# Banded prompt attention with the two key blocks packed into one, and attention traced beside its own projection

## The chip, the cores and the metric

The kernel runs on one NeuronCore of a Trainium2 chip. Its time is what the device takes for one execution, in microseconds (us). TensorE (PE in the profile; PEld is its weight load), VectorE (DVE), ScalarE (ACT) and GpSimd (POOL) compute; SyncE (SP) issues most of the DMA transfers, in order. The four compute engines each run their instructions in a fixed order and meet through semaphores.

## The reference

One inference step of a hybrid decoder layer over a prompt of 2048 tokens (and 8 single decode tokens beside it), model width 1024, in float32:

- n = RMSNorm(x); one projection u = n @ w_in gives for attention q (8 heads of 64), k and v (2 key-value heads of 64), and for the gated linear attention (GLA) q, k, v, an output gate r (512 wide) and a low-rank decay input (16 wide).
- Attention: q and k are RMS-normed per head. A query at position t sees the keys t-127 to t. In blocks of 128 tokens, query i of a block sees key j of its own block if j <= i, and key j of the block before if j > i. The score is q.k/8 plus a bias by distance (one of 32 buckets, per head); a learned sink per head joins the softmax as one more score without a value.
- GLA: a chunked exact recurrence with a data-dependent decay, then a norm per head and multiplication with silu(r).
- h = x + [attention | GLA] @ w_o, then y = h + (silu(z @ w_gate) * (z @ w_up)) @ w_down with z = RMSNorm(h).

The two conditions j <= i and j > i complement each other: for each pair (i, j) exactly one of the two key blocks counts. So 128 scores per query and head carry everything that 256 masked ones carry (in the first block there is no block before).

## The kernel before

The prompt is 16 blocks of 128 tokens (`NB`, `P`). The kernel has stages: A (projection for attention and r, and attention), B (GLA), the output projection, and the feed-forward part. Only stage A changes. Float32 products are made of three products of a high and a low part (`mm3`, lines 102 to 106, hence PE lines 104 to 106 for all dense products); `split` (lines 91 to 93) makes the parts with an ACT copy (line 92) and a DVE subtraction (line 93).

Stage A has these functions:

- `front(b)` loads a block of x, norms it, transposes it on PE and splits it into `nT`; two `nT` buffers exist. It also stores `nT` to DRAM (`nT_d`) for stage B.
- `project(b)` makes q (512 wide) and k, v and decay input (272 wide) with the weights `WA`: 24 PE products for each. q and k are normed (POOL squares, DVE sums, `rstd_fast`), transposed by PE and split into `qT` and `kT`. `kT` holds 256 keys: the own block in its second half, and the block before, copied there by POOL, in its first.
- `project_r(b)` makes r (512 wide) with the weights `WR`: 24 products, then `gate_r` (ACT copy, POOL, three ACT functions, POOL) and a store to `r_d`.
- `attend(b)`, for each of two groups of four heads: scores of 128 queries against 256 keys, two heads to a PSUM bank (`scp`, one bank); DVE adds the bias, which is minus 1e30 outside the band, and takes the maximum (line 360); ACT exponentiates and sums (line 367); POOL divides (line 372). Then for each of the two key blocks PE transposes the four heads' probabilities into a bank (`ppp`, two banks; line 383), `split` takes them to `pT`, and two products with v accumulate in `po` (lines 387 and 388). The result is stored to `mix_d` (line 391). Score buffers `S` are 128 x 1024, three of them; the weight loads at the start use the same buffers for staging.
- `make_bias` builds the bias for 256 keys from 32 buckets at the start, `decode_a` is a generator that does the decode tokens' attention in pieces between the blocks.

The order of the instructions on each engine isn't the traced order as such: a planner orders them by a simulated timeline (`schedule_with_timeline_sim=True`), in which the traced order is the priority. In the loop over blocks (lines 534 to 554) the traced order is front(b+2), project(b+1), project_r(b+1), attend(b); the r products of the last two blocks stand behind the loop. Stage B's buffers lie over those of stage A and come free one by one (`reuse_waits="tile"`). Stage B begins with its own weight loads (`wrq` line 632, `wrb` line 625), the load of `zT` from `nT_d` (line 671) and the q and k products `ps_qk` (line 685) with their copies to `qTb` and `kTb` (lines 687 and 689); later it loads the r blocks from `r_d` (line 741).

## Time and profile before

| what | value |
|---|---|
| median of 3 runs | 2298.53 us (2294.03 to 2301.5) |
| the profiled execution's own time | 2301.44 us |
| its span | 2299.7 us |
| mean granted TensorE clock | 0.984 |
| DMA moved | 364.35 MB |

The page gives for each engine its busy time and share of the span; PE busy isn't PE at its peak, since matmuls are pipelined. Grouped rows read: line, engine, operation, output <- inputs, shape, count, then busy us and mean ns of one, then the idle time of the engine just before them and what ended it. In timelines a row begins with its start and duration in us.

### The profile page before, as it was taken

How to read it: one execution, taken by the hardware profiler on the slowest of the kernel's cores; microseconds unless marked ns; L12 is line 12 of the kernel's file. 1: busy time of each engine (PE TensorE's matmuls, PEld its weight loads, DVE VectorE, ACT ScalarE, POOL GpSimd, SP SyncE). 2: the span in 40 equal slices, each digit the busy share in tenths (PEclk: the TensorE clock that was granted, in tenths of full speed). 3: DMA queues.
4: the chain of work that ended last, by engine and by line, in shares of the span. 5: the costliest groups of instructions: out<-in, count | busy, mean ns of one | idle time of the engine just before them, and what ended most of it. 6: DMA issues, size and time to landing. Idle time of an engine off the chain costs nothing.

```text
span 2299.7 us, 34866 instructions
## 1 busy us (share of the span) xinstructions
PE 2223.9 (97%) x12649; PEld 1921.5 (84%) x12649; DVE 1597.5 (69%) x3241; ACT 955.6 (42%) x2121; POOL 627.8 (27%) x799
## 2 busy tenths in 40 slices
PE   8999998899998899999999999999999999999997
PEld 6888886788887788688888889999999968787886
DVE  6787887588676466766666767666676675748487
ACT  5666777343443233423333323333333243434342
POOL 2443443455465133311110111111010122222222
PEclk9999998999998999999999999999999999999999
DMA  7323334245424699863333357323232378878777
GB/s 240 122 77 111 94 102 157 92 138 171 143 88 184 237 293 317 303 202 110 92 112 94 103 186 277 98 88 107 87 115 88 106 212 174 218 168 218 166 206 239
DMA packets 211225, 364.35 MB, mean 158 GB/s; under 512 B 15428, under 2 KB 128349, under 8 KB 207965
## 3 DMA queue, kind: packets, MB, share of 16 engines
q1 hardware_dynamic: 173996, 258.65, 34.6%
q0 software_dynamic: 37056, 103.47, 17.7%
q8 instruction: 100, 1.64, 0.3%
q14 instruction: 73, 0.59, 0.1%
HBM read 210.98 MB, written 152.16 MB: 158 GB/s over the span
## 4 chain that ended last, share of the span: by engine, by line
PE 81%; DVE 5%; DMA 5%; issue 4%; POOL 2%; ACT 2%; SPq 0%; POOLq 0%; DVEq 0%; ACTq 0%
PE ps_b L105 7%; PE ps_b L104 7%; PE ps_b L106 7%; PE ps_c L105 5%; PE ps_c L104 5%; PE ps_c L106 5%; PE ps_a L105 5%; PE ps_a L104 5%; PE ps_a L106 5%; PE ps_d L104 3%; PE ps_wo L104 3%; PE ps_d L106 3%; PE ps_d L105 3%; PE ps_wo L106 3%; PE ps_wo L105 3%
## 5 line engine op out<-in xcount | busy, mean ns | idle before, releaser
L104 PE MATMUL ps_b<-z,whl 128*128 128x258 f32 (+1 forms) x792 | 254.0, 321 | 1.2 <-ACT whl L92 1.2
L106 PE MATMUL ps_b<-z,whl 128*128 128x258 f32 (+1 forms) x792 | 253.1, 320 | 1.7 <-DVE whl L93 1.7
L105 PE MATMUL ps_b<-z,whl 128*128 128x258 f32 (+1 forms) x792 | 254.3, 321 | 0.0
L92 ACT CAST dm<-mr 128x384 fp32r<-128x384 f32 (+1 forms) x224 | 108.1, 488 | 187.2 <-PE ps_b L106 99.4
L105 PE MATMUL ps_a<-z,whl 128*128 128x258 f32 (+1 forms) x528 | 169.2, 320 | 0.0
L105 PE MATMUL ps_c<-z,whl 128*128 128x258 f32 (+1 forms) x528 | 169.1, 320 | 0.0
L106 PE MATMUL ps_a<-z,whl 128*128 128x258 f32 (+1 forms) x528 | 168.9, 320 | 0.0
L106 PE MATMUL ps_c<-z,whl 128*128 128x258 f32 (+1 forms) x528 | 168.9, 320 | 0.0
L104 PE MATMUL ps_c<-z,whl 128*128 128x258 f32 (+1 forms) x528 | 168.6, 319 | 0.2 <-DMA z<-zc_d_P 0.2
L104 PE MATMUL ps_a<-z,whl 128*128 128x258 f32 (+1 forms) x528 | 168.8, 320 | 0.0
L106 PEld LDWEIGHTS ps_b<-z,whl 128*128 128x128 f32 x792 | 149.4, 189 | 14.5 <-DVE whl L93 2.4
L104 PEld LDWEIGHTS ps_b<-z,whl 128*128 128x128 f32 x792 | 149.4, 189 | 13.1 <-ACT whl L92 1.3
L105 PEld LDWEIGHTS ps_b<-z,whl 128*128 128x128 f32 x792 | 149.3, 189 | 11.9
L93 DVE TENSOR_TENSOR dm<-mr,dm 128x384 fp32r<-128x384 f32 (+1 forms) x224 | 115.1, 518 | 59.6 <-ACT dm L92 59.6
L92 ACT CAST whl<-wrg 128x512 fp32r<-128x512 f32 x132 | 81.6, 619 | 156.7 <-PE ps_b L106 82.2
L802 POOL TENSOR_TENSOR bd<-E,qTb 64x128 f32<-64x128 f32 x224 | 126.7, 566 | 60.7 <-ACT E L787 47.2
L969 DVE TENSOR_TENSOR gu<-ps_c,gu 128x512 f32<-128x512 f32 (+1 forms) x130 | 78.0, 600 | 57.8 <-PE ps_c L106 57.2
L93 DVE TENSOR_TENSOR whl<-wrg,whl 128x512 fp32r<-128x512 f32 x132 | 90.7, 688 | 36.6 <-ACT whl L92 36.3
L1268 POOL DMA_DIRECT2D md_d<-m x22 | 15.6, 711 | 363.8 <-DVE m L1231 363.8
L92 ACT CAST whl<-sy 128x512 fp32r<-128x512 f32 x88 | 54.6, 620 | 134.7 <-PE ps_b L106 84.7
L104 PE MATMUL ps_wo<-WO,mt 128*128 128x512 f32 x256 | 103.6, 404 | 6.9 <-ACT mt L92 6.9
L104 PEld LDWEIGHTS ps_c<-z,whl 128*128 128x128 f32 x528 | 99.8, 189 | 8.6 <-issue 0.6
(390 smaller groups left out, 6669.1 us busy)
## 6 DMA issues: line engine op xcount, KB each, us to landing
mr<-md_d SPq DMA_DIRECT2D x24, 1344.0 KB
zc_d_P<-zhl POOLq DMA_DIRECT2D x56, 512.0 KB, 6.4
z<-zc_d_P SPq DMA_DIRECT2D x14, 2048.0 KB
wrg<-in_w_gate_dram SPq DMA_DIRECT2D x44, 512.0 KB
wrg<-in_w_up_dram SPq DMA_DIRECT2D x44, 512.0 KB
nT_d<-nT SPq DMA_DIRECT2D x16, 1024.0 KB
zT<-nT_d SPq DMA_DIRECT2D x8, 2048.0 KB
h_d<-gu POOLq DMA_DIRECT2D x48, 256.0 KB, 4.6
```

The source lines that it names most:

```text
L92: nc.scalar.copy(h, src)
L93: (eng or nc.vector).tensor_tensor(l, src, h.bitcast(F32), ALU.subtract)
L104: nc.tensor.matmul(ps, lh, rh, start=start, stop=False, skip_group_check=more)
L105: nc.tensor.matmul(ps, lh, rl, start=False, stop=False, skip_group_check=more)
L106: nc.tensor.matmul(ps, ll, rh, start=False, stop=stop, skip_group_check=more)
L802: nc.gpsimd.tensor_tensor(bv[rows, :, h], eo, qo, ALU.mult)
L969: nc.vector.tensor_tensor(out, a, b, ALU.add)
L1268: nc.gpsimd.dma_start(md_d[sb][g][:, :, q, fp - GROUPS[g][0], :], src.rearrange("p (m t) -> p m t", m=4))
```

## The change

1. Scores are packed. After the score products of a pair of heads (still 256 keys wide), a predicated copy on DVE writes, where j > i (`afterQ`), the score of the earlier block's key over that of the own block's key, within the PSUM bank. In the first block it writes minus 1e30 from the tile `none`. Bias, maximum, exponential and division then go over 128 keys in place of 256, and the bias needs no mask.
2. The products with v change: with p the packed probabilities, v the own and v' the earlier values, the sum is p v + (p where j > i)(v' - v). So p is transposed once per head group and split once; POOL multiplies both parts with the mask `afterK` into `pa`; two products use `vp`, two use `dv`, which `project` makes with a POOL subtraction and a split. There are four products per head group, as before.
3. `S` has six buffers of half the size; the weight loads are staged in pieces of 512 elements where they use them. The score pool has two banks, the transpose pool one.
4. The loop's traced order is front(b+1), project(b), attend(b), project_r(b). The r products of blocks 11 to 15 are traced later: 11 in block 13, 12 and 13 in block 14, 14 and 15 in block 15, each behind attend. They load their `nT` again from `nT_d` (1 MB).

```diff
+LATE = (11, {13: (11,), 14: (12, 13), 15: (14, 15)})
...
-        sp = pool(ph, "a_s", 3)
+        sp = pool(ph, "a_s", 6)
...
-        scp = pool(ph, "a_sc", 1, space=PSUM)
-        ppp = pool(ph, "a_pp", 2, space=PSUM)
+        scp = pool(ph, "a_sc", 2, space=PSUM)
+        ppp = pool(ph, "a_pp", 1, space=PSUM)
...
+        def staged_split(hi, lo, src, width):
+            nk = src.shape[1]
+            staged[0] += 1
+            if staged[0] % 2 == 0 and nk * width > 512:
+                wr = wl.tile([P, D], F32, tag="pT", name="wr", bufs=3).rearrange("p (k n) -> p k n", n=width)
+                nc.sync.dma_start(wr, src)
+                split(hi, lo, wr)
+                return
+            step = min(512 // width, nk)
+            for k in range(0, nk, step):
+                wr = sp.tile([P, 512], F32, tag="S", name="wr")[:, 0:step * width].rearrange("p (k n) -> p k n", n=width)
+                nc.sync.dma_start(wr, src[:, k:k + step])
+                split(hi[:, k:k + step], lo[:, k:k + step], wr)
...
+            vraw[b] = vsrc
+            if b:
+                dv = wk.tile([P, 2, HD], F32, tag="dv", name="dv", bufs=1)
+                nc.gpsimd.tensor_tensor(dv, vraw.pop(b - 1), vsrc, ALU.subtract)
+                d4 = dvs[b % 3].rearrange("p v (a d) -> p (v a) d", d=HD)
+                split(d4[:, 0:4:3], d4[:, 1:3], dv)
...
         def project_r(b):
-            pr = dense(nTs.pop(b), P, WR, 0, 512)
+            if b in nTs:
+                nT = nTs.pop(b)
+            else:
+                nT = nTp.tile([P, 2, KD, P], F32R, tag="nT", name="nTr")
+                nc.sync.dma_start(nT.bitcast(F32), nT_d[b // 2][:, :, :, (b % 2) * P:(b % 2 + 1) * P])
+            pr = dense(nT, P, WR, 0, 512)
...
-                St = sp.tile([P, 4, 256], F32, tag="S", name="S")
+                St = sp.tile([P, 4, P], F32, tag="S", name="S")
...
+                    pv = ps.rearrange("p (c a j) -> p c a j", c=2, a=2)
+                    other = pv[:, :, 0] if b else none.unsqueeze(1).to_broadcast([P, 2, P])
+                    nc.vector.copy_predicated(pv[:, :, 1], afterQ.unsqueeze(1).to_broadcast([P, 2, P]), other)
...
-                        nc.vector.tensor_tensor_reduce(St[:, c, k0:], ps[:, o:o + nk], bias[:, h, k0:], 1.0,
+                        nc.vector.tensor_tensor_reduce(St[:, c], ps[:, o + P:o + 256], bias[:, h], 1.0,
...
-                for kt in kts:
-                    ps = ppp.tile([P, 512], F32, tag="pp", name="ps_p")
-                    for c in range(4):
-                        nc.tensor.transpose(ps[:, c * P:(c + 1) * P], S[v][:, c, kt * P:(kt + 1) * P], ident)
-                    pT = wl.tile([P, 2, 512], F32R, tag="pT", name="pT", bufs=3)
-                    split(pT[:, 0], pT[:, 1], ps)
-                    vv = vps_ if kt == 0 else vp
-                    nc.tensor.matmul(po, vv[:, v], pT[:, 0], start=kt == kts[0], stop=False)
-                    nc.tensor.matmul(po, vv[:, v], pT[:, 1], start=False, stop=kt == 1)
+                ps = ppp.tile([P, 512], F32, tag="pp", name="ps_p")
+                for c in range(4):
+                    nc.tensor.transpose(ps[:, c * P:(c + 1) * P], S[v][:, c], ident)
+                pT = wl.tile([P, 2, 512], F32R, tag="pT", name="pT", bufs=3)
+                split(pT[:, 0], pT[:, 1], ps)
+                if b:
+                    pa = wl.tile([P, 2, 512], F32R, tag="pT", name="pa", bufs=3)
+                    for i in range(2):
+                        nc.gpsimd.tensor_tensor(pa[:, i].rearrange("p (c t) -> p c t", c=4),
+                                                pT[:, i].bitcast(F32).rearrange("p (c t) -> p c t", c=4),
+                                                afterK.unsqueeze(1).to_broadcast([P, 4, P]), ALU.mult)
+                for i in range(2):
+                    nc.tensor.matmul(po, vp[:, v], pT[:, i], start=i == 0, stop=i == 1 and b == 0)
+                if b:
+                    for i in range(2):
+                        nc.tensor.matmul(po, dv[:, v], pa[:, i], start=False, stop=i == 1)
...
-            if b + 2 < NB:
-                front(b + 2)
             if 1 < b + 1 < NB:
-                project(b + 1)
-                if b + 1 < NB - 2:
-                    project_r(b + 1)
+                front(b + 1)
+            if b > 1:
+                project(b)
             attend(b)
+            if b >= LATE[0]:
+                nTs.pop(b)
+            elif b > 1:
+                project_r(b)
+            for late in LATE[1].get(b, ()):
+                project_r(late)
...
-        project_r(NB - 2)
-        project_r(NB - 1)
```

What else moves with it: the bias table has 256 columns in place of 384 and is built by two flips in place of four; the masks are loaded as `c_after` (two of 128 x 128); `ks` has three buffers, since v of the block before is needed; the decode tokens' square goes to a `pT` buffer.

More of the change, by code (lines that the diff above doesn't have):

```diff
@@ L216, in hymba_kernel @@
             vps.append(vp)
+        dvs = [pc.tile([P, 2, P], F32R, name=f"dv{i}") for i in range(3)]
+        vraw = {}
         def dense(nT, n, W, c0, c1):
@@ L366, in attend @@
                     h = 4 * v + c
[L367 removed]
+                    nc.scalar.activation(St[:, c], St[:, c], AF.Exp, bias=nm[:, h:h + 1],
                                          accum_out=den[:, h:h + 1])
@@ L1386, in _onehot @@
 def _onehot():
-    m = np.arange(384)
-    dist = 255 - m
-    n = np.maximum(dist, 0)
+    m = np.arange(256)
+    n = (127 - m) % 128
     nf = np.maximum(n, 1).astype(np.float32)
```

85 lines of the change are left out of this document (40 added, 45 removed).

## The prediction

> **What bounds the kernel now.** I read the page's totals first, then the busy time by stretch, then the PE timeline of the one stretch where PE isn't full, then the grouped instructions for prices. The times are of one profiled execution: 2301.44 us, of which the span is 2299.7.
>
> ```profile
> span 2299.7 us, 34866 instructions
> PE 2223.9 (97%) x12649; PEld 1921.5 (84%) x12649; DVE 1597.5 (69%) x3241; ACT 955.6 (42%) x2121; POOL 627.8 (27%) x799
> ```
>
> PE is the busiest engine, but the share is over all stages; the change lies in stage A (prompt projection and attention) alone. In the view by stretch the columns are stretch, length, then busy us of PE, PEld, DVE, ACT, POOL, the granted TensorE clock, DMA share, GB/s:
>
> ```profile
> 60.00:340.00 280.00, 280.00 (x1680) 243.16 (x1679) 226.27 (x634) 199.94 (x550) 121.83 (x115) 1.00 0.33 101
> ...
> 356.00:372.00 16.00, 9.62 (x43) 6.89 (x42) 12.18 (x41) 11.98 (x34) 4.58 (x3) 0.79 0.22 58
> 372.00:390.00 18.00, 13.11 (x87) 11.98 (x88) 16.11 (x42) 15.02 (x39) 8.43 (x4) 0.90 0.84 276
> 390.00:410.00 20.00, 16.50 (x100) 14.09 (x100) 10.64 (x34) 11.40 (x33) 7.71 (x9) 0.92 0.08 28
> ...
> 500.00:600.00 100.00, 95.82 (x620) 84.04 (x619) 81.49 (x181) 43.80 (x104) 54.97 (x80) 1.00 0.51 161
> ```
>
> From 60 to 340 us PE has no idle time at all and DVE, the next, is at 226.3/280 = 81%. So in this body a PE instruction taken away is time gained, and DVE work only counts once it passes PE's. From 356 to 410 PE idles (54 - 39.2 = 14.8 us) and is granted less clock: 9.62 x 0.21 + 13.11 x 0.10 + 16.50 x 0.08 = 4.6 us more. That tail holds 19.4 us which better order can win. What PE does there (start, duration, then the idle time before it in brackets):
>
> ```profile
> 364.04 0.58 PE L355 MATMUL ps_s<-kT,qT 128*128 128x256 f32 x1 [2.27 <-DVE mx L360]
> ...
> 365.06 0.80 PE L387 MATMUL po<-pT,vp 128*128 128x512 f32 x1
> ...
> 371.87 0.39 PE L104 MATMUL ps_qk<-zT,W 128*128 128x264 f32 x1 [0.29 <-DVE qT L315]
> ...
> 374.77 0.28 PE L106 MATMUL ps_qk<-zT,WQ 128*128 128x264 f32 x1
> ...
> 383.23 0.58 PE L355 MATMUL ps_s<-kT,qT 128*128 128x256 f32 x1 [2.99 <-DVE mx L360]
> ```
>
> It runs score products that wait for VectorE to empty the one score bank, with nothing beside them. Why so many attentions are left there, the SP queue shows (issue of each store and load):
>
> ```profile
> 323.58 0.33 SPq L335 DMA_DIRECT2D r_d<-r  x1
> 325.72 0.32 SPq L391 DMA_DIRECT2D mix_d<-o  x1
> ...
> 347.82 0.33 SPq L391 DMA_DIRECT2D mix_d<-o  x1
> ...
> 365.35 0.32 SPq L335 DMA_DIRECT2D r_d<-r  x1
> ...
> 370.34 0.42 SPq L391 DMA_DIRECT2D mix_d<-o  x1
> ...
> 383.52 0.34 SPq L335 DMA_DIRECT2D r_d<-r  x1
> 387.90 0.80 SPq L673 DMA_DIRECT2D lrTb<-lr_d  x2
> 390.35 0.34 SPq L391 DMA_DIRECT2D mix_d<-o  x1
> ...
> 403.41 6.88 SPq L391 DMA_DIRECT2D mix_d<-o  x2
> ```
>
> Of 16 r products only two stores follow the one at 323.58, so 14 are done; of 16 attentions five stores follow 325.72, so 11 are done. The attentions, each traced behind the next block's projection, trail by three blocks, and the tail is made of them.
>
> **The change, part by part.**
>
> ```profile
> 215.14 0.87 PE ps_p L383 x8
> ...
> 223.10 0.23 PE ps_d L105
> ```
> ```profile
> L383 PE MATMUL ps_p<-ident,S x248: 270/272/421, 60.3 to 405.7; 128*128 128x128 f32 x124
> ```
> ```profile
> L104 PE MATMUL ps_d<-WR,nT 128*128 128x512 f32 x106 | 42.2, 398 | 0.0
> L360 DVE CUSTOM_DVE_ANT_0 S<-ps_s,bias,sinkB 128x256 f32<-128x256 f32 x97 | 43.2, 479 | 11.6 <-PE ps_s L356 11.0
> L93 DVE TENSOR_TENSOR pT<-ps_p,pT 128x512 fp32r<-128x512 f32 x48 | 31.8, 683 | 3.1 <-ACT pT L92 2.7
> L93 DVE TENSOR_TENSOR vp<-ks,vp 128x128 fp32r<-128x128 f32 x12 | 7.0, 587 | 3.8 <-ACT vp L92 3.8
> L372 POOL TENSOR_TENSOR S<-S,den 128x1024 f32<-128x1024 f32 x23 | 43.6, 1895 | 70.7 <-DVE den L371 29.5 <-DVE rf_t L125 10.4 <-DVE rf_t L124 10.3
> L240 POOL TENSOR_SCALAR rt<-r 128x512 f32<-128x512 f32 x12 | 18.0, 1496 | 42.0 <-ACT r L239 42.0
> L251 POOL TENSOR_TENSOR sq<-qs 128x512 f32<-128x512 f32 x14 | 15.0, 1074 | 6.6 <-ACT qs L289 6.6
> L241 ACT ACTIVATE rt<-rt 128x512 f32<-128x512 f32 x12 | 7.6, 633 | 1.2 <-POOL rt L240 1.2
> ```
> ```profile
> L360 DVE CUSTOM_DVE_ANT_0 S<-ps_s,bias,sinkB 128x128 f32<-128x128 f32 x8 | 2.4, 339 | 2.6 <-PE ps_s L356 2.6
> L513 PE MATMUL ps_rev<-rev,flip 128*128 128x512 f32 x8 | 4.2, 612 | 0.2 <-DVE bias L514 0.2
> ```
> ```profile
> L815 DVE COPY_PREDICATED AT<-lmask,ps_l 128x512 f32<-128x512 uint8 x41 | 37.0, 902 | 9.1 <-PE ps_l L807 8.9
> ```
>
> *PE.* The durations overlap in the pipe, so PE is priced by spacing, from the chain: eight transposes take 0.87 us (0.109 each), a 512-wide product 0.23. Transposes of the probabilities fall from 248 to 16 x 8 = 128: 120 x 0.109 = **-13.1 us**, in the full body or in the tail. The score products keep their width; the products with values stay four per head group (two with v, two with the differences dv). Halving the bias drops 4 of 8 flip records: between 0 (VectorE work and weight loads set that early stretch) and 4 x 0.612 = -2.4 us; I take **-1**.
>
> *DVE.* 106/8 = 13.25 r products lie in the stretch of those rows, nearly all of the 280 us: a block is 21.1 us of PE, 226.3/13.25 = 17.1 of DVE. Per block the change takes away 8 x (0.479 - 0.339) = 1.1 and two splits of 0.683, and adds one 128x128 subtraction (0.587) and four predicated copies 2x128 wide from PSUM to PSUM, a form the trace lacks. Bounds: 0.339 (the 128-wide reduction) and 0.902 (the 512-wide predicated copy); I take 0.48, the 256-wide PSUM reduction, since the width is that. DVE: 17.1 - 1.1 - 1.4 + 0.6 + 1.9 = 17.1 us (16.6 to 18.8) against PE's 21.1 - 0.9 = 20.2. Cost: nothing, behind PE.
>
> *ACT* loses two 512-wide casts and half of each exponential per block; it stays below its 200/280. *POOL* loses half of two normalisations (1.9 us), gains four 512-wide mask products (4 x 1.07 = 4.3) and a small subtraction: about 121.8/13.25 = 9.2 to 12 us of 20.2. The two mask products stand between the split and the dv products of a head group, 2.1 us in a row; the first two value products don't wait for them. Cover is other blocks' dense products; without cover it is 2.1 us each.
>
> *Staging, constants, buffers.* Weight bytes are the same in smaller pieces, the rev loads shrink from four to two, two 64 KB masks come in, the decode square moves to another pool: zero, give or take 2 us. A second score bank takes away the waits seen at 364 and 383 us; a single transpose bank is emptied in 0.6 + 0.7 us twice per block, far below 20.
>
> *Order.* An attention now stands before the next projection, so at the last projection about one attention is left and not 4.5. r products 11 to 15 come at blocks 13 to 15. Each is 24 x 0.23 = 5.6 us of PE, with the copy, three activations, two POOL steps and the store as before, and a new 1 MB reload of the normalised block on SP. That is 28 us of PE work, independent of attention, to lie under the last chains: the 19.4 us go. What is late next is the last r product's own tail, because stage B's first copies already waited for it:
>
> ```profile
> 381.25 2.24 POOL L244 TENSOR_TENSOR r<-r,rt 128x512 f32<-128x512 f32 x1
> ```
> ```profile
> 389.30 0.68 ACT L687 ACTIVATE qTb<-ps_qk 128x264 f32<-128x264 f32 x2
> ```
>
> The first q product was complete at 375, its copy ran at 389.3, just after the last r buffer was stored (383.5) and freed (387.9): qTb lies over that memory. Now the chain starts when the last r product ends: copy 0.6, POOL 1.5, three activations 1.9, POOL 1.3 to 2.2, store 4.4 = about 10 us. Two q groups (24 in 371.87 to 374.9, 3 us) cover 6. Left over: 4 us, and a stretch at half clock behind it (365.06: 0.80, where a 512-wide product in the body has 0.40) of about 1.5. Net of the tail: -19.4 + 5.5 = **-13.9**.
>
> *Added cost.* Blocks 11 and 12 have no r product: PE 20.2 - 5.6 = 14.6 against DVE's 17.1, 2.5 us each: 0 to +5, I take **+3**. Reloads: SP issues in order, and each waits for a slot of two; behind it queue attention's stores and stage B's weight and zT loads, for which the q products wait.
>
> ```profile
> nT_d<-nT SPq DMA_DIRECT2D x16, 1024.0 KB
> ```
> ```profile
> 343.08 11.61 DMA wrq<-in_w_in_dram
> ```
>
> At 276 GB/s a megabyte takes 3.8 us, less than an r product: 0. At the 11.6 us which the piece in the chain took it is 6 us too long, four times: +24. I take **+2**, since the stretches have DMA room (0.22 to 0.84). Waits in the body from chains placed just in time: 0, as now, to 12 (stage B's 4.2 idle per 100 us, over 280); **+3**.
>
> Sum: -13.1 - 1 - 13.9 + 3 + 2 + 3 = -20. 2301.4 - 20 = 2281.4; the profiled run lies 2.9 above the median 2298.5 of the three shown, so **2278**.
>
> **The rivals.**
>
> *Order as before (0.15).* The instruction order is a planner's, by readiness; tracing attention earlier need not place it earlier. Then the tail stays and 14 us of PE work go: 2284. For it: score products already break into the middle of dense groups. Against: the three blocks of lag match the traced order.
>
> *POOL blocks VectorE (0.13).*
>
> ```profile
> L261 DVE TENSOR_TENSOR qn<-qs,rf_y x16: 674/691/2290, 25.5 to 351.2; 128x512 f32<-128x512 f32 x16
> ```
>
> One form goes from 0.67 to 2.29 us. If each of the four mask products and the subtraction delayed a DVE instruction by its own length (4.8 us a block), DVE were at 21.9 and would pass PE's 20.2: 11 blocks x 1.7 + 2 x 7 = 33 us in place of the 6 for waits and blocks 11 and 12, so -20 + 27 = +7, 2305; half of the 33, more likely, -20 + 10 = -10, 2288. Against: the median is 0.69, so most aren't delayed. The Trainium skill, SBUF — State Buffer, section SBUF: two separate sides, states such a lock: a GpSimd instruction and a VectorE one with two SBUF inputs exclude each other for the whole instruction. The maximum in the row agrees, the median says how seldom it bites.
>
> *Slower: PE waits in each block (0.14).* Attention now stands ahead of the next projection in the order PE must keep. If in each block one product waits on the longer DVE-ACT-POOL chain as at 364.04 (2.27 us, then some 1.7 of half clock), that is 4 us x 14 = 56 in place of my 3: -20 + 53 = +33, 2331. It decides from 23/14 = 1.6 us per block on. For it: two mask products and a predicated copy lie in the chain. Against: PE waits for nothing in 280 us now, with the same engines behind it.
>
> **How the numbers follow.** The forecast has 0.58: with nothing added and no wait for the last r it would be -35 (2264), with waits of 12, blocks of 5 and half the reload bound -2, so its own range is 2264 to 2294. What a measurement can tell from no change is 0.3%, 6.9 us. Faster: 0.50 of the forecast, 0.15 of the first rival, 0.06 of the second: 0.71. Same: 0.07 + 0.06: 0.13. Slower: the third rival's 0.14 and 0.01 of each of the two. The range to 2301 takes in most of the second rival and leaves out the slower one.
>
> **What would show it.** 128 transposes of S; no PE idle in the body, blocks of about 20 us; the r stores 11 to 15 behind the 13th attention's, at most two mix stores after the last projection; a q-copy wait of about 4 us. Wrong would be: PE waits on pa or den in mid-body, a predicated copy near 0.9, PE waiting on the reload, DVE over 90%.

## The result, and the profile after

The changed kernel takes 2318.76 us (median of 4 runs, 2315.1 to 2325.28), the kernel before 2299.04 beside it: a ratio of 1.0082, 95% interval 1.0064 to 1.01. It is slower by 19.7 us, where 20 us less were forecast. The profiled execution took 2315.1 us, the fastest of the four, so the two profiles read here lie 13.7 us apart and not 19.7. Of all runs in this document one, of e16, ran in a slower state of the chip (2438.13 us at a granted clock of 0.842), and e16's numbers leave it out.

The page's totals of the changed kernel:

```profile
span 2313.3 us, 34767 instructions
...
PE 2215.2 (96%) x12525; PEld 1907.2 (82%) x12525; DVE 1605.9 (69%) x3294; ACT 933.0 (40%) x2111; POOL 685.2 (30%) x874
```

PE has less work, as planned: 12525 instructions, 124 fewer, and 8.7 us less busy time. So the loss is in waiting and in the slower clock beside it. Four stretches of stage A in the view by stretch (stretch, length, busy us of PE, PEld, DVE, ACT, POOL, granted clock, DMA share, GB/s), the kernel before first and the changed one behind it:

```profile
40.00:100.00 60.00, 59.53 (x330) 48.07 (x329) 45.29 (x134) 41.68 (x115) 26.01 (x27) 1.00 0.43 130
100.00:250.00 150.00, 150.00 (x903) 130.52 (x902) 118.39 (x333) 103.02 (x281) 65.55 (x63) 1.00 0.30 92
250.00:340.00 90.00, 90.00 (x551) 79.36 (x550) 76.69 (x215) 68.32 (x189) 39.37 (x37) 1.00 0.35 108
340.00:430.00 90.00, 74.81 (x405) 61.63 (x404) 62.71 (x184) 55.60 (x145) 34.43 (x35) 0.91 0.46 147
```
```profile
40.00:100.00 60.00, 50.91 (x240) 37.61 (x240) 37.69 (x111) 35.22 (x95) 25.90 (x28) 0.86 0.34 102
100.00:250.00 150.00, 148.09 (x867) 127.28 (x866) 121.22 (x375) 95.58 (x289) 86.63 (x92) 1.00 0.31 98
250.00:340.00 90.00, 82.31 (x480) 71.08 (x480) 80.78 (x234) 58.50 (x180) 52.21 (x58) 0.96 0.33 104
340.00:430.00 90.00, 72.05 (x385) 60.87 (x385) 59.49 (x162) 49.99 (x136) 47.93 (x45) 0.92 0.58 178
```

I read such a row as *lost time*: length minus PE's busy time, plus busy time times what the clock lacks to 1. For the first row of the changed kernel that is 9.1 + 0.14 x 50.9 = 16.2 us. By stretch:

| stretch | before | after |
|---|---|---|
| 40 to 100 | 0.5 | 16.2 |
| 100 to 250 | 0 | 1.9 |
| 250 to 340 | 0 | 11.0 |
| 340 to 430 | 21.9 | 23.7 |
| sum | 22.4 | 52.8 |

30.4 us more are lost, and 13.1 us of work are gone: 17.3 us net. Where stage A ends shows the same. The groups of the first value product of stage B (the start of the first and the last stand behind the durations), before and after:

```profile
L104 PE MATMUL ps_v<-WV,zT x128: 388/396/795, 410.4 to 715.8; 128*128 128x512 f32 x128
```
```profile
L106 PE MATMUL ps_v<-WV,zT x128: 388/395/629, 428.2 to 729.8; 128*128 128x512 f32 x128
```

It comes 17.8 us later. At the last value product 14.0 us are left (729.8 against 715.8); how stage B wins back the rest wasn't followed. So there are two new holes, one at the start, one from 250 us on, and the old hole at the end of stage A is as large as it was.

*The hole from 250 us on.* PE's longest waits from 250 to 430 us in the changed kernel (who waited for what: sum, times, longest), and two of them in PE's timeline:

```profile
PE ps_d L106 <- DMA nTr<-nT_d: 8.4, 2, 5.0
PE ps_s L380 <- ACT kT L344: 5.3, 3, 3.1
PE ps_k L340 <- DVE kn L283: 3.8, 2, 2.1
PE po L420 <- DVE pT L95: 3.5, 1, 3.5
```
```profile
349.85 0.80 PE L106 MATMUL ps_d<-WR,nTr 128*128 128x512 f32 x1 [5.04 <-DMA nTr<-nT_d]
365.58 0.50 PE L106 MATMUL ps_d<-WR,nTr 128*128 128x512 f32 x1 [3.35 <-DMA nTr<-nT_d]
```

The r products that were to fill the end wait for their own reload, and run slowly behind the wait (0.80 for a product that takes 0.39). SP's queue shows when the reloads (`nTr`) were issued:

```profile
306.71 0.53 SPq L297 DMA_DIRECT2D nT_d<-nT  x1
312.63 0.59 SPq L358 DMA_DIRECT2D nTr<-nT_d  x1
...
343.53 0.59 SPq L358 DMA_DIRECT2D nTr<-nT_d  x1
344.57 1.81 SPq L297 DMA_DIRECT2D nT_d<-nT  x1
346.47 3.89 SPq L361 DMA_DIRECT2D r_d<-r  x1
...
359.26 0.58 SPq L358 DMA_DIRECT2D nTr<-nT_d  x1
```

The first reload goes out at 312.6 and the second at 343.5, 31 us apart. The buffers are the two that the last blocks' norms also use. PE starts its last projection product with block 13 at 312.31 and with block 14 at 343.22, so each of these reloads goes out as a projection lets go of its buffer; the other way round, ACT begins block 15's norm at 332.0, just after PE has read the first reloaded block (331.1). The last projection ends at 383.5, by when three of the five late r stores (346.47, and others at 367.54 and 380.42) have gone, and PE ends the fifth late r product at 396.6, before the last block's first score product at 399.69: these r products ran ahead of the last attention and not beside it.

*The hole at the start.* PE's timeline there, start, duration, then idle time in brackets and what ended it:

```profile
75.14 0.47 PE L420 MATMUL po<-pT,vp 128*128 128x512 f32 x1 [1.47 <-ACT rt L256]
...
79.26 1.22 PE L420 MATMUL po<-pT,vp 128*128 128x512 f32 x2 [1.39 <-DVE o L425]
...
83.63 1.02 PE L141 MATMUL ps_nT<-ident,xtd 8*128 8x8 f32 x8 [1.04 <-DVE xtd L136]
85.77 1.11 PE L141 MATMUL ps_nT<-ident,xt 128*128 128x128 f32 x4 [1.12 <-DVE nTdec L95]
```

No dense product stands between these: PE has run out of normed blocks, because the next block's transposes come behind the decode tokens' (`xtd`). A smaller part of the 16.2 us lies before that: PE waits for the load of the bias to be flipped, which is issued at 42.28 us where the first of these loads went out at 36.06 before. PE's row of that wait in the kernel before, in the changed one and in e17 (below):

```profile
48.94 1.13 PE L513 MATMUL ps_rev<-rev,flip 128*128 128x512 f32 x2 [0.16 <-DVE bias L514]
```
```profile
46.02 1.58 PE L552 MATMUL ps_rev<-rev,flip 128*128 128x512 f32 x2 [2.86 <-DMA rev<-ext_d]
```
```profile
46.82 1.10 PE L557 MATMUL ps_rev<-rev,flip 128*128 128x512 f32 x2 [3.20 <-DMA rev<-ext_d]
```

The prediction had PE waiting on the reload among its signs of being wrong; the hole at the start it hadn't named.

### The profile page after: what moved, and what is told of

The parts are those of the page before. It is cut to its first block, busy times and chain, and to the rows that moved or that the text cites. A ratio compares the mean times of both kernels' runs of the same rounds, so it can differ in the third digit from the quotient of the medians.

```text
span 2313.3 us, 34767 instructions
## 1 busy us (share of the span) xinstructions
PE 2215.2 (96%) x12525; PEld 1907.2 (82%) x12525; DVE 1605.9 (69%) x3294; ACT 933.0 (40%) x2111; POOL 685.2 (30%) x874
## 3 DMA queue, kind: packets, MB, share of 16 engines
q0 software_dynamic: 37056, 103.47, 17.7%
## 4 chain that ended last, share of the span: by engine, by line
PE 62%; issue 16%; DVE 7%; POOL 7%; DMA 5%; ACT 2%; SPq 1%; POOLq 0%; DVEq 0%; ACTq 0%
PE ps_b L107 5%; PE ps_b L106 5%; PE ps_b L108 5%; PE ps_c L107 4%; PE ps_c L106 4%; PE ps_c L108 4%; POOL h_d L1406 4%; PE ps_a L107 3%; PE ps_a L106 3%; PE ps_a L108 3%; PE ps_wo L106 3%; PE ps_wo L108 3%; PE ps_wo L107 3%; PE ps_d L106 2%; PE ps_d L108 2%
```

## The experiments

Times are medians, ratios are against runs of the kernel before beside them, whose medians were 2299.8 to 2301.0.

### Which part costs: e1 to e4

e1: arithmetic, buffers and banks of the changed kernel, the loop's traced order of before.

```diff
-            if 1 < b + 1 < NB:
-                front(b + 1)
-            if b > 1:
-                project(b)
+            if b + 2 < NB:
+                front(b + 2)
+            if 1 < b + 1 < NB:
+                project(b + 1)
+                if b + 1 < NB - 2:
+                    project_r(b + 1)
             attend(b)
...
+        project_r(NB - 2)
+        project_r(NB - 1)
```

> Packed keys, buffers and banks of the changed kernel, but the traced order of the kernel before (next block's projection and r product ahead of each attention, the last two r products behind the loop, nothing reloaded). If the new order is what loses time, PE is busy without a gap again from 60 us to the last projection, the 120 transposes are gone, the tail stays: about 2299 - 13 = 2286. If the packed arithmetic loses it (predicated copies, POOL masks, VectorE and POOL blocking each other), PE waits in the body here too: 2305 to 2320.

Measured: 2294.41 us, ratio 0.9972 (0.9962 to 0.9982). It lies between the two expected times.

e2: the changed kernel, each r product with its own block.

```diff
-LATE = (11, {13: (11,), 14: (12, 13), 15: (14, 15)})
+LATE = (16, {})
```

> The changed kernel with every r product right behind its own attention, none late and none reloaded. If the late r products cost more than they fill (8.4 us of waits for the reload, VectorE-bound blocks 11 and 12, about 11 us of lost PE time from 250 to 340 us), this is 5 to 15 us faster than the changed kernel, 2304 to 2314, and the 16 us lost before 100 us stay. If they do fill the tail, it is slower than the changed kernel by 10 us or more, about 2330.

Measured: 2300.25 us, ratio 1.0 (0.999 to 1.0009). Late r products cost 18.5 us in place of filling the end, more than the 5 to 15 expected.

e3: the changed kernel, in which blocks 0 and 1 are projected in the loop as the others are, so that no two attentions follow each other at the start.

```diff
-        project(0)
-        project(1)
-        project_r(0)
-        project_r(1)
         dec = decode_a()
...
-            if b > 1:
-                project(b)
+            project(b)
```

> The changed kernel, but the first two blocks go through the loop like the others (projection, attention, r product), in place of two projections and two r products ahead of two attentions in a row. If the 16 us of PE time lost from 40 to 100 us come from the two attentions in a row with too little dense work beside them, most of it goes: 2305 to 2310. If they come from the decode piece or from the loads at the start, the time stays at 2319.

Measured: 2322.45 us, ratio 1.0097 (1.0082 to 1.0112). The hole at the start doesn't come from the two attentions in a row.

e4: the arithmetic, buffers and banks of before with the order, the late r products and their reload as in the change.

```diff
+LATE = (11, {13: (11,), 14: (12, 13), 15: (14, 15)})
...
-            if b + 2 < NB:
-                front(b + 2)
             if 1 < b + 1 < NB:
-                project(b + 1)
-                if b + 1 < NB - 2:
-                    project_r(b + 1)
+                front(b + 1)
+            if b > 1:
+                project(b)
             attend(b)
+            if b >= LATE[0]:
+                nTs.pop(b)
+            elif b > 1:
+                project_r(b)
+            for late in LATE[1].get(b, ()):
+                project_r(late)
```

> The kernel before with nothing changed but the traced order: front, projection, attention, r product of the same block, five r products late with a reload; 256 keys, old buffers and banks. If the order is what loses time, the loss of about 33 us shows here without the 13 us that packing saves: 2325 to 2335. If the packed arithmetic is what loses it, the order gains as forecast: 2280 to 2290.

Measured: 2322.92 us, ratio 1.0097 (1.0082 to 1.0112). That is just under the range expected if the order loses the time. The order with its late r products costs some 23 us with either arithmetic. So the loss comes with the order, and the packing as it stands in e1 wins 6.5 us, less than its 14 us of PE work; e9 below shows why.

### The hole at the start: e5, e6, e9, e10, e12

e5 is e1, e6 the changed kernel, with the decode pieces begun one block later.

```diff
-            if b >= 1:
+            if b >= 2:
                 next(dec, None)
```

> The packed arithmetic in the order of before (2294.4 us), with one edit: the decode tokens' pieces begin after block 2 in place of block 1. Nothing is left out. Theory: the loss of about 9 us between 60 and 100 us comes from the first decode piece, whose square now takes a pT buffer, waits there for the packed block's last products, and holds the next block's norm behind it on ScalarE; by then two more blocks are in flight and the wait is covered. Then the loss in that stretch falls from 9.0 to under 3 us and the time to 2286 to 2289. Rival: the packed chain itself is too long for the first blocks, whatever stands beside it; then the loss stays at 7 to 10 us and the time at 2292 to 2296.

> The changed kernel (2318.8 us) with the same edit: the decode pieces begin after block 2. Theory, the decode piece is what starves TensorE at the start: the loss between 40 and 100 us falls from 16 to under 7 us and the time to 2308 to 2311. Rival, the start starves because only one block is normed ahead (front of b+1, not of b+2): the loss stays at 12 to 17 and the time at 2315 to 2320.

Measured: e5 2298.45 (0.9996, 0.9983 to 1.0009), e6 2320.27 (1.0088, 1.0072 to 1.0105). Neither theory: nothing was won, but the hole moved with the piece. In e5 nothing is lost from 60 to 100 us any more and 11.6 us from 100 to 150; in e6 9.7 us are lost from 40 to 100 and 10.8 from 100 to 250, in place of 16.2 and 1.9. So it belongs to the decode piece, wherever that stands.

The next three put its square back where it was, into a score buffer: e9 is e1, e10 the changed kernel and e12 is e2 with this edit.

```diff
-                sqd = wl.tile([P, D], F32, tag="pT", name="sqd", bufs=3)
+                sqd = sp.tile([P, D], BF16, tag="S", name="sqd")
```

> The packed arithmetic in the order of before (2294.4 us), with the decode tokens' square put back among the score buffers S (stored as bfloat16, so that it fits into one; nothing reads it). Nothing is left out. With the decode pieces begun a block later the loss of 9 us at 60 to 100 us moved to 100 to 150 (0.0 and 11.6), so it belongs to the decode piece. Theory A, it is the square's wait for a pT buffer: the loss between 40 and 150 us falls from 12.8 to under 5 us and the time to 2286 to 2290. Theory B, it is VectorE's and ScalarE's full order around the piece, whatever the buffer: the loss stays at 9 to 15 us and the time at 2292 to 2297.

> The changed kernel (2318.8 us) with the decode square back among the score buffers S. Theory A (the square's pT buffer): the loss between 40 and 150 us falls from 18 to under 9 us, the time to 2307 to 2312. Theory B (the order around the piece): 2315 to 2321.

> The changed kernel without late r products (2300.3 us) and with the decode square among the S buffers. Theory A (the square's pT buffer): 2289 to 2293. Theory B: 2297 to 2302. The difference to the old order with the same edit is the price of attention ahead of the next projection: some 6 us if the two effects add.

Measured: e9 2285.21 (0.9935, 0.9918 to 0.9951), e10 2306.82 (1.0029, 1.0019 to 1.004), e12 2292.09 (0.9963, 0.995 to 0.9976). Theory A in all three, in e9 and e10 just below its range: 9.2, 12.0 and 8.2 us won. The square's own group (count, durations, first and last start) in the changed kernel, and then in e10:

```profile
L133 ACT ACTIVATE sqd<-xtd x1: 1051/1051/1051, 78.4 to 78.4; 8x1024 f32<-8x1024 f32 x1
```
```profile
L133 ACT ACTIVATE sqd<-xtd x1: 1052/1052/1052, 63.8 to 63.8; 8x1024 bf16<-8x1024 f32 x1
```

It takes the same 1.05 us and starts 14.6 us earlier. The edit changes the buffer (and the type of an output that nothing reads); so what counts is the ring it is in, here the three `pT` buffers, which the attentions fill with `pT` and `pa` at that time. ACT has no idle time just ahead of the square at 78.4: it stands late in ACT's order. That the planner put it there because a `pT` buffer came free late fits all this, but isn't shown directly. Right behind it on ACT stands the next block's norm (79.44 us, in e10 64.86), and behind that the transposes on PE. e10 loses, by this row, 2.9 us from 40 to 100 in place of 16.2, all of it the wait for the flip's load (the second row is for the late r products below, as is the third):

```profile
40.00:100.00 60.00, 57.13 (x334) 46.90 (x333) 49.23 (x155) 42.12 (x122) 32.22 (x34) 1.00 0.42 130
...
250.00:340.00 90.00, 78.81 (x453) 67.88 (x452) 82.03 (x250) 58.68 (x187) 52.16 (x57) 0.93 0.41 124
340.00:430.00 90.00, 77.44 (x380) 64.76 (x380) 54.57 (x140) 45.49 (x113) 42.28 (x43) 0.88 0.55 172
```

One thing stays open: e4 keeps the square in one of three full-size score buffers and has a hole of 12.8 us from 60 to 100 us too. Its square starts at 72.3 us, earlier than in the kernel before (77.5), which has no hole there; so a late square alone doesn't explain it, and nothing else was tried.

### The late r products: e7, e8, e17

e7 is the changed kernel with only the r products of blocks 14 and 15 late, from normed blocks that stay in SBUF.

```diff
-LATE = (11, {13: (11,), 14: (12, 13), 15: (14, 15)})
+LATE = (14, {})
...
-            if b >= LATE[0]:
-                nTs.pop(b)
-            elif b > 1:
+            if 1 < b < LATE[0]:
                 project_r(b)
...
+        project_r(NB - 2)
+        project_r(NB - 1)
```

> The changed kernel, but r of blocks 11 to 13 stays with its block, and only the r products of blocks 14 and 15 are traced behind the loop, with their normed blocks still in SBUF: no reload, no block without an r product before the 14th. Nothing is left out. Without any late product the time was 2300.3. Theory A, the late products cost through the reload (8 us of waits on it) and the stretches without r: the time is 2293 to 2301, since two r products cover part of the 16 us which TensorE loses at the end. Rival B, any r product behind the last attention delays the memory that the next stage needs: 2305 to 2315.

Measured: 2302.02 us, ratio 1.0009 (0.9999 to 1.0019), the same as without late products (e2). It is just above theory A's range. Two late products without a reload cost next to nothing, and win nothing.

e8 has all five behind the last attention.

```diff
+LATE = (11, {15: (11, 12, 13, 14, 15)})
```

> The changed kernel with all five late r products (11 to 15, reloaded) traced behind the last attention, none between the last projections. Nothing is left out. Theory A, the five cost because blocks 11 to 15 without r products are bound by VectorE and then each waits on a reload that goes through the two buffers one after the other: the time is 2318 to 2332, with the loss between 250 and 390 us larger than in the changed kernel (about 25). Rival B, they cost because they ran ahead of the last projections and so covered nothing: 2300 to 2308.

Measured: 2308.85 us, ratio 1.0037 (1.0026 to 1.0048): 9.9 us under the changed kernel, 8.6 over e2, just past rival B's range. So both theories held half: that three of them ran ahead of the last projections, with their reloads, was some 10 us of the cost, and 8.6 remain when they don't. Its row from 250 to 340 us shows a loss that isn't a wait on the reload, for e8 issues its first reload at 336 us:

```profile
250.00:340.00 90.00, 80.51 (x478) 69.26 (x477) 82.34 (x239) 58.27 (x182) 52.50 (x57) 0.96 0.32 99
```

It loses 12.7 us there, and the changed kernel 11.0. These blocks have no r product beside them. So a reload that comes late costs in two ways: PE waits for it, and more blocks go without an r product.

e17 is e10, in which the reloads of blocks 11, 12 and 14 have a buffer of their own, in the memory that the decode work has left.

```diff
-                nT = nTp.tile([P, 2, KD, P], F32R, tag="nT", name="nTr")
+                if not late_pool:
+                    late_pool.append(pool(ph, "a_nTr", 1))
+                nT = (late_pool[0].tile([P, 2, KD, P], F32R, tag="nTr", name="nTr") if b in (11, 12, 14)
+                      else nTp.tile([P, 2, KD, P], F32R, tag="nT", name="nTr"))
```

> The changed kernel with the decode square among the S buffers (2306.8 us), with an own buffer for the reloaded blocks 11, 12 and 14 (in the memory that the decode tokens' work has left by then), while 13 and 15 reload into the two buffers as before. Nothing is left out. Theory A, TensorE loses 8.8 us of waits on the reload, and some 5 more of clock behind them, because the reload queues for the two buffers which the last norms use: the waits fall under 2 us and the time to 2294 to 2299. Theory B, the late products cost because they run ahead of the last projections and so hold up the last chains, whenever they are loaded: 2303 to 2309.

Measured: 2285.88 us, ratio 0.9942 (0.9926 to 0.9959). 20.9 us under e10, far more than theory A's 8 to 13. PE's longest waits from 250 to 430 us in e17 (the reload is none of them), its first two reloads in SP's queue, and its rows by stretch:

```profile
PE ps_s L385 <- ACT kT L344: 6.8, 3, 4.7
PE ps_v L781 <- ACT v L777: 1.4, 1, 1.4
```
```profile
266.07 0.59 SPq L363 DMA_DIRECT2D nTr<-nT_d  x1
...
308.99 0.59 SPq L363 DMA_DIRECT2D nTr<-nT_d  x1
```
```profile
250.00:340.00 90.00, 85.79 (x510) 74.44 (x509) 80.75 (x256) 58.73 (x191) 55.17 (x60) 1.00 0.48 141
340.00:430.00 90.00, 79.99 (x477) 67.47 (x476) 68.27 (x165) 48.70 (x120) 57.22 (x65) 0.96 0.58 186
```

The first reload goes out at 266 us, an r product is there from 300 us on to stand between the waits, and what is lost falls from 16.7 to 4.2 us (250 to 340) and from 21.9 to 13.2 (340 to 430): 21.2 us, as much as the medians differ (20.9; the two profiles differ by 24.0). Of it 9.5 us are idle time of PE (11.2 + 12.6 in e10, 4.2 + 10.0 here; e10's waits on the reload were 8.8), and 11.6 are clock (0.07 x 78.8 + 0.12 x 77.4 = 14.8 in e10, 0.04 x 80.0 = 3.2 here). So by these rows the slower clock cost rather more than the idle time.

Against e12, which has no late products, e17 wins 6.2 us by the medians; the intervals of the two ratios overlap a little. So much the five late r products are worth when their reload doesn't share the norms' buffers.

### What the packing is worth: e11, e14, e13

e11 is e9 with the banks of before, e14 the kernel before with the banks of the change.

```diff
-        scp = pool(ph, "a_sc", 2, space=PSUM)
-        ppp = pool(ph, "a_pp", 1, space=PSUM)
+        scp = pool(ph, "a_sc", 1, space=PSUM)
+        ppp = pool(ph, "a_pp", 2, space=PSUM)
```

e14's edit is the reverse one.

> As the run of the old order with the square among the S buffers, and with one score bank and two transpose banks, as before the change. Theory, the second score bank wins what TensorE waits for VectorE's score maxima: with one bank the time is 4 to 10 us longer than with two. Rival, the single transpose bank costs as much as the second score bank wins: within 3 us of it.

> The kernel before, with one edit: two score banks and one transpose bank in place of one and two. Nothing is left out. Theory A, the second score bank is worth its 18 us whatever the arithmetic: 2282 to 2288. Theory B, the bank pays only with the packed scores, where one group of four heads needs one transpose bank and not two: 2296 to 2310, since two transposed key blocks per group then share one bank.

Measured: e11 2303.43 (1.0014, 1.0004 to 1.0023), e14 2329.76 (1.0126, 1.011 to 1.0142). PE waits in e11, from 250 to 430 us:

```profile
PE ps_s L380 <- DVE mx L389: 6.1, 4, 2.3
```

| | one score bank, two for transposes | two score banks, one for transposes |
|---|---|---|
| arithmetic of before | 2300.4 and 2301.0 (before) | 2329.8 (e14) |
| packed | 2303.4 (e11) | 2285.2 (e9) |

Neither half wins alone; e11 is 18.2 us above e9 where 4 to 10 were expected, and e14 lies above both its ranges. From 250 to 430 us PE waits 7.2 us for the maxima in the kernel before and 0.9 in e14, but for the transposed probabilities and the outputs (`pT`, `o`) 2.2 before and 18.7 in e14. A reading that fits: packed scores hold their bank longer, by a predicated copy ahead of the maxima, and so need two; and only packed probabilities, which are transposed once per head group and not twice, leave a transpose bank over. Together they are worth 15.2 us, close to the 14.1 of PE work forecast.

e13 is e9 with the four mask products of a block on VectorE.

```diff
-                        nc.gpsimd.tensor_tensor(pa[:, i].rearrange("p (c t) -> p c t", c=4),
+                        nc.vector.tensor_tensor(pa[:, i].rearrange("p (c t) -> p c t", c=4),
```

> The packed arithmetic in the old order with the decode square among the S buffers (2285.2 us), with the four mask products of a block moved from GpSimd to VectorE. Nothing is left out. VectorE is busy 206.6 of the 240 us from 100 to 340 there, with 11 blocks in them. Theory, GpSimd holds up VectorE's instructions with two inputs in SBUF: GpSimd loses 43 products of 1.33 us (57 us) and VectorE gains 43 of about 0.68 (29 us), but its small instructions (den, nm, es, kn, rf) become shorter by 15 to 25 us in sum, so that its busy time is 210 to 221 and the time stays within 4 us of 2285. Rival, GpSimd holds up nothing: VectorE's busy time rises by the whole 29 us to 235 of 240, and the time becomes 2292 to 2305.

Measured: 2285.43 us, ratio 0.9931 (0.991 to 0.9952), the same as e9. The view by stretch and some groups of VectorE from 100 to 340 us, e9 first and then e13 (groups: busy us, mean ns, then idle time before them):

```profile
100.00:340.00 240.00, 237.15 (x1402) 205.07 (x1400) 206.56 (x613) 159.77 (x478) 147.17 (x153) 1.00 0.31 99
```
```profile
L95 DVE TENSOR_TENSOR pT<-ps_p,pT 128x512 fp32r<-128x512 f32 x21 | 14.4, 684 | 2.0 <-ACT pT L94 1.6
...
L399 DVE TENSOR_TENSOR den<-den,es 128x4 f32<-128x4 f32 x22 | 5.5, 250 | 11.1 <-ACT es L398 11.1
...
L95 DVE TENSOR_TENSOR dv<-dv,dv 128x128 fp32r<-128x128 f32 x11 | 5.3, 485 | 0.3 <-ACT dv L94 0.3
...
L123 DVE TENSOR_SCALAR rf_v<-ssq 128x2 f32<-128x2 f32 x11 | 5.2, 470 | 0.2
```
```profile
100.00:340.00 240.00, 238.97 (x1413) 206.58 (x1412) 216.40 (x662) 160.92 (x485) 104.02 (x114) 1.00 0.33 103
```
```profile
L416 DVE TENSOR_TENSOR pa<-pT,afterK 128x512 fp32r<-128x512 f32 x42 | 33.2, 797 | 0.0
...
L95 DVE TENSOR_TENSOR pT<-ps_p,pT 128x512 fp32r<-128x512 f32 x22 | 15.1, 686 | 3.0 <-ACT pT L94 2.9
...
L399 DVE TENSOR_TENSOR den<-den,es 128x4 f32<-128x4 f32 x23 | 3.6, 158 | 5.3 <-ACT es L398 5.2
L95 DVE TENSOR_TENSOR dv<-dv,dv 128x128 fp32r<-128x128 f32 x11 | 3.1, 281 | 0.0
...
L123 DVE TENSOR_SCALAR rf_v<-ssq 128x2 f32<-128x2 f32 x11 | 2.3, 210 | 0.2
```

VectorE gets 33.2 us of mask products and is busy only 9.8 us longer: its other instructions became 23.4 us shorter, 2.1 per block. So GpSimd does hold up VectorE, as the second rival said, but in this order it isn't on the path.

### Towards a version that beats both: e15, e16, e18

e15 is e9 with the r product of block b+1 traced behind the attention of block b; the projection stays ahead of it.

```diff
             if 1 < b + 1 < NB:
                 project(b + 1)
-                if b + 1 < NB - 2:
-                    project_r(b + 1)
             attend(b)
+            if 1 < b + 1 < NB - 2:
+                project_r(b + 1)
```

> The packed arithmetic in the old order with the decode square among the S buffers (2285.2 us), with one edit: in each turn of the loop the r product of block b+1 is traced behind the attention of block b, in place of before it; the projection of b+1 stays ahead of the attention. Theory A, attention ahead of the next projection is what costs the 6.9 us of the new order, through TensorE's waits on that projection's k chain: here these are absent and the time is 2279 to 2287. Theory B, any attention that stands earlier displaces cover: 2289 to 2295.

Measured: 2281.43 us, ratio 0.9923 (0.9902 to 0.9943), the best of all: 19.6 us under the kernel before in the same runs. Against e9 it is 3.8 us lower, but the two intervals overlap. This is within theory A's range: attention may come early, so long as the next projection stands ahead of it. e12, in which the projection (and the last two r products) stand otherwise, takes 10.7 us more. e15's last stretch loses 13.1 + 0.06 x 76.9 = 17.7 us:

```profile
340.00:430.00 90.00, 76.87 (x457) 65.49 (x457) 73.49 (x180) 47.95 (x125) 58.13 (x64) 0.94 0.48 157
```

e16 is e15 with the mask products on VectorE, e18 is e15 with a third r product at the end, for which block 15 is normed into an own buffer. e16's edit is that of e13; e18's is

```diff
+            if b == NB - 1:
+                nT = pool(ph, "a_nTl", 1).tile([P, 2, KD, P], F32R, name="nT")
...
-            if 1 < b + 1 < NB - 2:
+            if 1 < b + 1 < NB - 3:
                 project_r(b + 1)
...
+        project_r(NB - 3)
```

> The packed arithmetic, decode square among the S buffers, projection of b+1, attention of b, r product of b+1 (2281.4 us), and the four mask products of a block on VectorE in place of GpSimd. Nothing is left out. In the other order the move to VectorE changed nothing (2285.2 and 2285.4). Theory, the mask products are off the path in the body and shorten the chain by about 1.1 us per head group in the tail: 2277 to 2281. Rival, VectorE at 85 to 90% leaves no room for it: 2282 to 2288.

> As the order with the r product behind attention (2281.4 us), with three r products in place of two behind the loop (13 joins 14 and 15), all from normed blocks that stay in SBUF: the norm of block 15 goes into an own buffer. Nothing is left out. Theory A, 5.6 us more of work that needs no attention cover part of the 17.5 us that TensorE loses from 340 to 430: 2275 to 2279. Theory B, the last block's chains run ahead of it anyway, and one more r product at the end delays the next stage: 2281 to 2288.

Measured: e16 2290.69 (0.9955, 0.9937 to 0.9973), e18 2288.02 (0.9949, 0.9934 to 0.9964). e16 lies above both its ranges, e18 at the upper edge of theory B's. Neither wins over e15; the move to VectorE, which was free in e9's order, is 9 us worse here, and why was not pursued.

## Why the prediction was wrong, point by point

The whole difference is 19.7 + 20 = 39.7 us against the forecast. The first four points, and the flips in the fifth, are the steps that failed.

1. **"Reloads: ... I take +2."** They cost 20.9 us (e10 against e17). The working priced the transfer, and named the slot in half a sentence ("each waits for a slot of two") without pricing it. The slot was the price: the two buffers belong to blocks 13 and 14 until 312 and 343 us, so PE stood idle for the r product, ran slowly around that, and had more blocks without an r product; how the 20.9 us split between these isn't shown. That the bound of +24 was nearly reached is luck, for it priced a slow transfer. Mis-sized by 18.9 us.
2. **"... the decode square moves to another pool: zero, give or take 2 us."** It cost 12.0 us (the changed kernel against e10; 9.2 in the old order, 8.2 without late products). The instruction costs 1.05 us in both places. What was not asked is who holds the new buffer at that time and what then stands behind the square in ACT's order.
3. **"That is 28 us of PE work ... to lie under the last chains: the 19.4 us go."** Even with a free buffer for the reload, 13.2 us stay lost from 340 to 430 (e17) of 21.9 before: 8.7 won where 13.9 net was forecast. In the changed kernel none: 23.7. That only two attentions are left behind the last projection came true (their stores go out at 392.76 and 429.36 us); that the late r products lie under their chains did not.
4. **Waits in the body, +3, and r-free blocks, +3.** e17, whose order is that of the change, loses 4.2 us from 250 to 340, where its blocks without r products lie. That is near the forecast only because its reload comes early: e8 loses 12.7. From 100 to 250 it loses 4.5 us, so together some 3 more than the 6 allowed. The 3.2 us from 40 to 100 are the wait for the flip's load:

```profile
40.00:100.00 60.00, 56.77 (x331) 46.80 (x331) 48.97 (x153) 41.36 (x117) 31.56 (x34) 1.00 0.43 131
100.00:250.00 150.00, 145.47 (x846) 124.19 (x844) 122.30 (x360) 96.71 (x288) 90.58 (x94) 1.00 0.29 91
```

In times: points 1 and 2 make 18.9 + 12.0 = 30.9 us. e17, which has neither, is 15.2 us under the kernel before, where the working without its reload term says 22: 6.8 us short. The last 2.0 of the 39.7 are the shift of the kernel before between the runs (2299.0 and 2301.0). By the rows, points 3 to 5 come to some 5.2 + 2.7 + 3.2 = 11 us, more than the 6.8, so some 4 us were won where the working had nothing; where is open.

5. **Transposes, -13.1: right; the flips, -1: not.** The page's group has 128 transposes. The four flips fewer were priced as PE work, but PE now waits 2.86 us for the load that they need (3.20 in e17), where it waited 0.16. With banks and order set apart (e9) the kernel gains 15.2 us, and its stage A ends at 397.1 in place of 410.4.
6. **The second score bank and the single transpose bank: half right.** With the packed arithmetic the exchange of a transpose bank for a second score bank is worth 18.2 us (e11 against e9), which the working had inside the tail, and the single transpose bank is no limit there; with the arithmetic of before the same exchange costs 28.7 us (e14).
7. **The predicated copy, 0.48 us, was right (0.42), the mask product, 1.07, was short (1.32), and VectorE's 17.1 us a block was short by at most 1.** Groups of the changed kernel from 100 to 340 us:

```profile
L385 DVE COPY_PREDICATED ps_s<-afterQ,ps_s 128x256 f32<-128x256 uint8 x44 | 17.8, 421 | 6.0 <-PE ps_s L381 5.8
```
```profile
L416 POOL TENSOR_TENSOR pa<-pT,afterK 128x512 fp32r<-128x512 f32 x42 | 54.9, 1320 | 17.8 <-ACT pT L94 13.5 <-DVE pT L95 2.5 <-DVE rf_v L123 1.5
```

VectorE's busy time from 100 to 340 went from 118.39 + 76.69 = 195.1 (before) to 206.6 (e9), 1.0 per block if eleven are counted in both; but e9 does 88 of each score product in that time where before did 82, so part of it is more work done. e13 shows that delays by GpSimd are in it too.

8. **The rivals.** *Order as before* is out: the late r products did run where they were traced, which was the trouble. *POOL blocks VectorE* is there and has no price in time (e13). *PE waits in each block* gave the right side, and its 2331 is nearer than the forecast, but not for its reason: e17 loses 4.5 us in seven blocks from 100 to 250, 0.6 a block, where the rival decides from 1.6. What the new order costs without late products is 6.9 us (e12 against e9; the r products stand otherwise too); only 1.5 us of it lie ahead of the first value product of stage B (398.6 against 397.1), where the rest lies is open. The kernel didn't lose in each block, but mostly at two places where a buffer was shared.
9. **The range.** Its upper end doesn't follow from its terms: waits of 12, blocks of 5 and half the reload bound make +1 in place of -2, which would be 2299.5; 2294 comes from neither. The measured time lies above all of these.

The same sum in measured parts, from the kernel before (2300.4 beside e9 to e12): packing with its banks -15.2, the new order without late products +6.9, late r products with a shared reload buffer +14.7, the decode square in `pT` +12.0: 2318.8. These are steps along one chain of runs and add up by construction; taken in other orders the square costs 9.2 or 8.2.

## What to carry to other kernels

When an edit moves a tile to another pool or adds a load into one, price the *slot*, not the instruction: who holds the buffers at that moment, when does the last of them come free, and what stands behind that instruction in its engine's order. Work that is to fill a hole must have its data ready before the hole begins; a filler that waits itself leaves the hole open and adds its own. And take the buffers that an edit frees and the buffers that it needs as one: the score bank and the transpose bank each lost alone and won together.

## What the runs showed of the hardware

- Here waits of PE cost more than their length. Behind the reload's wait of 5.04 us a product took 0.80 us in place of 0.39, the next eight started 0.43 us apart in place of 0.23, and the granted clock was 0.86 in the stretch from 40 to 100 us, in which PE was idle 9.1 of 60 us in pieces of at most 2.9 us: 7.1 us of the 16.2 lost there are clock.
- GpSimd lengthens some of VectorE's instructions: a 128x4 addition took 250 ns in the mean beside the mask products on GpSimd and 158 without them, a 128x2 instruction with a single tensor input (`rf_v`) 470 and 210. A 128x512 subtraction with one input in PSUM (`pT`) took 684 and 686, so nothing was lost there. It isn't so for every small form: a 128x2 product of two inputs (`rf_t`, line 127) took 273 beside them and 391 without. The Trainium skill, SBUF — State Buffer, section SBUF: two separate sides, has the port pair that both share locked for a whole instruction, by VectorE instructions with two SBUF inputs or in a two-port mode; the trace agrees for the addition and, by the absence of a delay, for the subtraction with an input in PSUM. `rf_v` has one tensor input, so by that section it would be of the second kind; no run here shows its mode.
- A predicated copy of 128x256 within PSUM took 0.42 us.
